# Which engine makes the low halves of three groups of weights in a two-layer hybrid encoder

## The chip, the cores and the metric

The kernel runs on one core of one Trainium2 chip. The metric is the device time of one execution in microseconds (us); the median of three runs before the change is 1833.69 us (1831.79 to 1833.77). Five engines matter: TensorE (PE in the profile, with its weight loads as PEld), VectorE (DVE), ScalarE (ACT), GpSimd (POOL) and SyncE (SP), which here only issues transfers. Each engine works through its own queue of instructions in order, and waits at an instruction until what that instruction needs is there.

## The reference, cut to what matters

Two layers, 512 tokens, 1024 channels. Each layer normalises its input, multiplies it by one wide matrix `w_in`, and feeds the columns to three token mixers whose results are gated and added; a feed-forward block and a gated input embedding follow.

```python
h = rmsnorm(x, norm_mix[i])
proj = h @ w_in[i]
qa, ka, va, glu_in, qc, kc, vc, gates = jnp.split(proj, SPLITS, axis=-1)
ya = diff_attention(qa, ka, va, ...)        # 4 heads, two softmaxes each
yb = conformer_conv(glu_in, ...)            # 31 taps
yc = neighbourhood_attention(qc, kc, vc, ...)   # 8 heads, "natten"
ga, gb, gc = jnp.split(jax.nn.sigmoid(gates), 3, axis=-1)
merged = ga * (ya @ w_br_a[i]) + gb * (yb @ w_br_b[i]) + gc * (yc @ w_br_c[i])
x = x + merged @ w_o[i]
```

All of it is float32.

## The kernel before, in words

Every matrix product runs on TensorE in three parts. An operand is split into a high half, which is the value rounded to the type float32r (fp32r in the profile), and a low half, which is the rest (value minus high half). `mm3` then adds high times high, high times low and low times high. A product with 1024 input channels is eight chunks of 128, so 24 matmuls of 128x512.

Weights come from memory in blocks of 128x1024 float32 (512 KB). `weights` (L162) does this for one block: a transfer on SyncE's queue into the tile `wr` (L167), a copy on ScalarE that makes the high half `wh` (L139, called by `split`), and a subtraction on VectorE that makes the low half `wl` (L153, `tt`, called by `split` at L158). There are two `wr` buffers and three each of `wh` and `wl`, and the whole is put ahead of other work by a priority offset of up to 400, so that a block is prepared while earlier ones are multiplied. The transfer of a block can start only when the low half of the block two before it has been made, because it reuses that `wr` buffer; it is issued from SyncE's queue, where the small copies that arrange queries and keys (`stack`, L582) and the loads of attention biases (L611) are issued too.

`gemm` (L177) multiplies one block and `proj` calls it for a 128-column piece of `w_in`. The name of the stage, `self.phase`, is the prefix of the tile names in the profile: `natten_wl` is the low half of a weight block that was prepared in the stage called natten. One layer runs through glu (the convolution's inputs), natten (queries and keys of four head pairs by `natten_in`, values by `natten_v`), diff (queries and keys of four heads by `diff_in`, values by `diff_v`), gatec (`gate_c`, eight pieces of the third gate), gateb, branchc, mergea, mergeb, wo, ffn and ple. The values' weights go through `values`, which calls `weights` itself and not `gemm`.

The order of TensorE's instructions is written out by hand: attention units (scores, transposes of the probabilities, products with the values) are inserted a number of ticks after the projections that feed them; one tick is four chunks. All other engines' queues are ordered by the framework's planner from its own estimate of times and the priorities. The convolution's taps (L156, `conv_z`, 31 for each of four channel groups in a layer) run on VectorE as background work: some are tied behind certain instructions of each stage (three after every query or key product of natten, one in diff, two in gatec).

VectorE's other work in the stages of the change: scaling the projections (`natten_t`, `gatec_x`), rotary embedding (`diff_rp`), low halves of queries, keys and probabilities (`natten_pt`, `diff_pt`, `natten_a`), bias and row minimum of the scores (L619, `natten_b`), row maxima (L815, `diff_s`), the mixture of the two softmaxes (`diff_a`) and the sum of the attention result (`natten_y`). The tiles named `_mm`, `_sc`, `_tr` and `_av` lie in PSUM, TensorE's result memory; all others lie in SBUF. GpSimd has little to do: it clears 64 columns of some probability tiles (L627) and raises the norms' mean squares to the power -0.5 (L207).

Of the kernel before, what the change touches and what calls it, by code (L numbers as in the profile page):

```python
# [11 lines left out]
F32 = mybir.dt.float32  # L12
F32R = mybir.dt.float32r
I32 = mybir.dt.int32
AF = mybir.ActivationFunctionType
ALU = mybir.AluOpType
# [4 lines left out]
P = 128  # L21
# [36 lines left out]
class Net:  # L58
# [100 lines left out]
        self.act(hi, src, AF.Copy)  # L159
        self.tt(lo, src, hi.bitcast(F32), ALU.subtract)  # L160

    def weights(self, ap, n):  # L162
        with self.tc.high_priority(offset=min(self.w_ahead, self.tc.cur_priority - self.p0)):
            raw = self.sb("wr", [P, 1024])
            hi = self.sb("wh", [P, 1024], F32R)
            lo = self.sb("wl", [P, 1024], F32R)
            self.nc.sync.dma_start(raw[:, :n], ap[:, :n])  # L167
            self.split(hi[:, :n], lo[:, :n], raw[:, :n])
        return hi, lo

    def mm3(self, out, wh, wl, ah, al, first, last):
# [2 lines left out]
        mm(out, wh, al, start=False, stop=False)  # L174
        mm(out, wl, ah, start=False, stop=last)  # L175

    def gemm(self, out, ap, acts, first=True, last=True):  # L177

        n = len(acts)
        for o in range(0, n, 8):  # L180
            c = min(8, n - o)
            wh, wl = self.weights(ap[:, o * P:(o + c) * P], c * P)
            for k in range(c):
                s = slice(k * P, (k + 1) * P)
                h = acts[o + k]
                h = h if isinstance(h, tuple) else (h[:, 0, :], h[:, 1, :])
                self.mm3(out, wh[:, s], wl[:, s], h[0], h[1],
                         first and o + k == 0, last and o + k == n - 1)
                self.chunk()
# [234 lines left out]
    def proj(self, col0, tag="mm"):  # L424
        if self.first:
            return self.first.pop(0)
        ps = self.ps(tag)
        self.gemm(ps, self.a["w_in"][self.i, col0 // P], self.h)
        return ps

    def glu(self, zs):
# [690 lines left out]
```

## Time and profile before

| what | value |
|---|---|
| median of three runs | 1833.69 us |
| the profiled execution's own time | 1832.91 us |
| its span, first to last instruction | 1831.1 us |
| mean granted TensorE clock | 0.999 |
| VectorE busy | 1204.7 us (66%) |
| ScalarE busy | 748.1 us (41%) |
| GpSimd busy | 23.5 us (1%), 56 instructions |
| transfers | 213.80 MB |

The numbers come from one execution. A timeline row gives the start in us, the duration in us, the engine, the line of the kernel, the operation, output and inputs, and in square brackets how long the engine had been idle before it and what ended that. A group row gives the number of instructions, their busy time in us, the mean of one in ns, and the idle time before them with its releasers. Matmuls overlap one another, so their durations are longer than the distance between them.

### The profile page before, as it was taken

Reading aid. Unit: us, or ns where it says so; the run is one execution under the profiler, and the core shown is the slowest. Engines: PE = TensorE matmul, PEld = TensorE weight load, DVE = VectorE, ACT = ScalarE, POOL = GpSimd, SP = SyncE. Lnnn points to the kernel's source line nnn. Section 1 sums busy time; section 2 is a strip of 40 time slices with the busy share of each in tenths; the row PEclk is TensorE's granted clock in tenths of the full one; section 3 lists DMA queues with packets and bytes.
Section 4 is the critical chain, followed back from the end, with each engine's and each line's share of the span. In section 5 each row is a group of like instructions: output and inputs, shape, how many; then the busy total and the mean of one; then the engine's idle time right before and its main releaser. Section 6 shows DMA issues by size and latency. Waiting matters only on the chain.

```text
span 1831.1 us, 23573 instructions
## 1 busy us (share of the span) xinstructions
PE 1815.5 (99%) x8796; PEld 1522.9 (83%) x8796; DVE 1204.7 (66%) x1977; ACT 748.1 (41%) x1280; POOL 23.5 (1%) x56
## 2 busy tenths in 40 slices
PE   9999999999999999999999999999999999999998
PEld 7888888888888888888888888888888888888887
DVE  7788888898544434444767878888985443344455
ACT  5466545334432223233525765442344322223343
POOL 0000000000000000000000000000000000000000
PEclk9999999999999999999999999999999999999999
DMA  5566541334322232222436655322243222322222
GB/s 198 164 189 179 154 118 47 104 103 131 122 93 103 80 113 96 93 90 91 147 114 190 177 157 145 104 69 95 97 150 114 93 93 83 112 102 87 91 90 92
DMA packets 84194, 213.80 MB, mean 117 GB/s; under 512 B 11632, under 2 KB 18928, under 8 KB 84080
## 3 DMA queue, kind: packets, MB, share of 16 engines
q1 hardware_dynamic: 83504, 211.60, 36.8%
q8 instruction: 70, 1.15, 0.2%
q10 hardware_dynamic: 576, 0.69, 0.1%
q14 instruction: 44, 0.36, 0.1%
HBM read 176.59 MB, written 4.19 MB: 99 GB/s over the span
## 4 chain that ended last, share of the span: by engine, by line
PE 91%; DVE 5%; ACT 2%; issue 1%; DMA 1%; SPq 0%; ACTq 0%; DVEq 0%; POOLq 0%; POOL 0%
PE ffn_mm L175 13%; PE ffn_mm L174 13%; PE ffn_mm L173 13%; PE mergea_mm L175 2%; PE mergea_mm L174 2%; PE mergea_mm L173 2%; PE gatec_mm L173 2%; PE wo_mm L174 2%; PE gatec_mm L174 2%; PE gatec_mm L175 2%; PE gateb_mm L174 2%; PE gateb_mm L175 2%; PE wo_mm L175 2%; PE gateb_mm L173 2%; PE wo_mm L173 2%; PE ple_mm L174 2%
## 5 line engine op out<-in xcount | busy, mean ns | idle before, releaser
L139 ACT ACTIVATE ffn_wh<-ffn_wr 128x1024 fp32r<-128x1024 f32 (+1 forms) x152 | 144.7, 952 | 511.4 <-issue 358.3
L173 PE MATMUL ffn_mm<-wo_h,ffn_wh 128*128 128x512 f32 x704 | 274.2, 390 | 0.0
L175 PE MATMUL ffn_mm<-wo_h,ffn_wl 128*128 128x512 f32 x704 | 273.9, 389 | 0.0
L174 PE MATMUL ffn_mm<-wo_h,ffn_wh 128*128 128x512 f32 x704 | 273.9, 389 | 0.0
L153 DVE TENSOR_TENSOR ffn_wl<-ffn_wr,ffn_wh 128x1024 fp32r<-128x1024 f32 (+1 forms) x152 | 164.9, 1085 | 129.4 <-ACT ffn_wh L139 129.4
L156 DVE SCALAR_TENSOR_TENSOR conv_z<-glu_z,pre_par,conv_z 128x512 f32<-128x512 f32 x240 | 179.2, 747 | 1.9
L174 PEld LDWEIGHTS ffn_mm<-wo_h,ffn_wh 128*128 128x128 f32 x704 | 132.1, 188 | 27.5
L173 PEld LDWEIGHTS ffn_mm<-wo_h,ffn_wh 128*128 128x128 f32 x704 | 132.1, 188 | 27.4
L175 PEld LDWEIGHTS ffn_mm<-wo_h,ffn_wl 128*128 128x128 f32 x704 | 132.1, 188 | 27.3
L153 DVE TENSOR_TENSOR ffn_t<-ffn_t,ffn_mm 128x512 f32<-128x512 f32 x44 | 30.3, 688 | 114.8 <-PE ffn_mm L175 114.7
L153 DVE TENSOR_TENSOR ffn_t<-ffn_mm,wo_r 128x512 f32<-128x512 f32 x44 | 30.4, 691 | 111.2 <-PE ffn_mm L175 111.2
L139 ACT ACTIVATE mergea_wh<-mergea_wr 128x1024 fp32r<-128x1024 f32 (+1 forms) x32 | 27.2, 849 | 94.1 <-PE mergea_mm L174 63.1
L173 PE MATMUL ffn_mm<-ffn_z,ffn_wh 128*128 128x512 f32 x160 | 62.2, 389 | 0.0
L174 PE MATMUL ffn_mm<-ffn_z,ffn_wh 128*128 128x512 f32 x160 | 62.2, 389 | 0.0
L175 PE MATMUL ffn_mm<-ffn_z,ffn_wl 128*128 128x512 f32 x160 | 62.2, 389 | 0.0
L173 PE MATMUL ffn_mm<-ffn_y,ffn_wh 128*128 128x512 f32 x160 | 62.2, 389 | 0.0
L174 PE MATMUL ffn_mm<-ffn_y,ffn_wh 128*128 128x512 f32 x160 | 62.2, 389 | 0.0
L175 PE MATMUL ffn_mm<-ffn_y,ffn_wl 128*128 128x512 f32 x160 | 62.2, 389 | 0.0
L139 ACT ACTIVATE diff_a<-diff_sc,diff_s 128x512 f32<-128x512 f32 x32 | 22.0, 689 | 70.7 <-DVE diff_s L815 70.7
L815 DVE TENSOR_REDUCE diff_s<-diff_sc 128x1 f32<-128x512 f32 x64 | 42.1, 685 | 5.4 <-PE diff_sc L725 5.3
L139 ACT ACTIVATE natten_wh<-natten_wr 128x1024 fp32r<-128x1024 f32 x24 | 25.5, 1061 | 47.9 <-PE glu_mm L174 19.9
L153 DVE TENSOR_TENSOR wo_x<-wo_x,ffn_mm 128x512 f32<-128x512 f32 x32 | 22.0, 688 | 34.1 <-PE ffn_mm L175 34.1
(442 smaller groups left out, 4630.9 us busy)
## 6 DMA issues: line engine op xcount, KB each, us to landing
ffn_wr<-w_fg SPq DMA_DIRECT2D x44, 512.0 KB, 3.2
ffn_wr<-w_fu SPq DMA_DIRECT2D x44, 512.0 KB, 3.2
ffn_wr<-w_fd SPq DMA_DIRECT2D x32, 512.0 KB, 3.5
natten_b<-bias SPq DMA_DIRECT2D x32, 256.0 KB, 3.4
natten_wr<-w_in SPq DMA_DIRECT2D x16, 512.0 KB, 3.6
diff_wr<-w_in SPq DMA_DIRECT2D x16, 512.0 KB, 3.9
gatec_wr<-w_in SPq DMA_DIRECT2D x16, 512.0 KB, 3.9
gateb_wr<-w_in SPq DMA_DIRECT2D x16, 512.0 KB, 3.2
```

Of the source, the lines that this page charges most:

```text
L139: i = self.nc.scalar.activation(out, in_, func, **kw)
L153: return self.nc.vector.tensor_tensor(out, a, b, op)
L156: return self.nc.vector.scalar_tensor_tensor(out, a, s, b, op0, op1)
L173: mm(out, wh, ah, start=first, stop=False)
L174: mm(out, wh, al, start=False, stop=False)
L175: mm(out, wl, ah, start=False, stop=last)
L815: nc.vector.tensor_reduce(out=m[:, u:u + 1], in_=sc, op=ALU.max, axis=AX.X, negate=True)
```

## The change

The weight blocks of natten's queries and keys, of the differential attention's queries and keys, and of the gates c get their low half from GpSimd instead of VectorE. The operation is the same (block minus high half). The high half stays on ScalarE. That is eight blocks in each of the three stages of a layer, 48 in all; the values' blocks and every other stage stay as they are.

```diff
-    def weights(self, ap, n):
+    def weights(self, ap, n, pool=False):
...
             self.nc.sync.dma_start(raw[:, :n], ap[:, :n])
-            self.split(hi[:, :n], lo[:, :n], raw[:, :n])
+            if pool:
+                self.act(hi, raw, AF.Copy)
+                self.nc.gpsimd.tensor_tensor(lo, raw, hi.bitcast(F32), ALU.subtract)
+            else:
+                self.split(hi[:, :n], lo[:, :n], raw[:, :n])
         return hi, lo
...
-    def gemm(self, out, ap, acts, first=True, last=True):
+    def gemm(self, out, ap, acts, first=True, last=True, pool=False):
...
-            wh, wl = self.weights(ap[:, o * P:(o + c) * P], c * P)
+            wh, wl = self.weights(ap[:, o * P:(o + c) * P], c * P, pool)
...
-        self.gemm(ps, self.a["w_in"][self.i, col0 // P], self.h)
+        self.gemm(ps, self.a["w_in"][self.i, col0 // P], self.h,
+                  pool=self.phase in ("natten", "diff", "gatec"))
```

In these stages a block always has 1024 columns, so the whole tile in the new branch is the same size as the slice in the old one.

## The prediction

> **What bounds the kernel now.** The page's first part gives the busy time of each engine, and the view by windows that of the two stretches in which the 48 blocks are used (natten, diff and gatec of each layer).
>
> ```profile
> PE 1815.5 (99%) x8796; PEld 1522.9 (83%) x8796; DVE 1204.7 (66%) x1977; ACT 748.1 (41%) x1280; POOL 23.5 (1%) x56
> ...
> 40.00:300.00 260.00, 257.26 (x1488) 223.49 (x1487) 219.22 (x457) 142.60 (x316) 5.15 (x17) 1.00 0.51 147
> 945.00:1207.00 262.00, 258.63 (x1492) 224.23 (x1491) 216.67 (x446) 142.38 (x316) 5.15 (x17) 1.00 0.50 143
> ```
>
> TensorE is busy 1815.5 of 1831.1 us, and its matmuls are untouched. So the change can win only where TensorE is idle: 260 - 257.26 = 2.74 us in the first stretch and 262 - 258.63 = 3.37 us in the second, **6.1 us together**, 0.33% of the time. VectorE is busy 219.22 of 260 us, 84%, so its queue can be late there. Next the view of waits, for TensorE alone, in the two stretches (total, times, longest).
>
> ```profile
> PE natten_av L663 <- DVE natten_y L153: 1.0, 3, 0.6
> PE natten_sc L725 <- DVE natten_s L619: 1.0, 1, 1.0
> PE diff_tr L211 <- DVE diff_pt L153: 0.6, 1, 0.6
> ...
> PE natten_av L663 <- DVE natten_y L153: 1.4, 4, 0.7
> PE natten_sc L725 <- DVE natten_s L619: 1.0, 1, 1.0
> PE diff_tr L211 <- DVE diff_pt L153: 0.6, 1, 0.6
> ```
>
> These make 5.6 us, all of them waits for VectorE: 2.4 for `natten_y`, 2.0 for `natten_s`, 1.2 for `diff_pt`. What put VectorE behind is read from the chain of waits, whose pieces with a low half of the 48 blocks are these (start, length).
>
> ```profile
> 96.39 1.13 DVE natten_wl L153
> ...
> 127.17 1.14 DVE diff_wl L153
> ...
> 136.56 1.14 DVE diff_wl L153
> ...
> 220.69 1.23 DVE gatec_wl L153
> ...
> 1001.43 1.23 DVE natten_wl L153
> ...
> 1017.68 1.23 DVE natten_wl L153
> ...
> 1033.15 1.14 DVE diff_wl L153
> ...
> 1042.55 1.14 DVE diff_wl L153
> ...
> 1127.04 1.23 DVE gatec_wl L153
> ```
>
> Nine of the 48 lie on the path that sets the end. The timeline shows the plainest case: a low half stands between two score instructions, and TensorE waits for the second because it needs the score buffer back.
>
> ```profile
> 136.48 1.22 DVE L153 TENSOR_TENSOR diff_wl<-diff_wr,diff_wh 128x1024 fp32r<-128x1024 f32 x1
> 137.62 0.41 DVE L619 CUSTOM_DVE_ANT_0 natten_b<-natten_sc,natten_b 128x256 f32<-128x256 f32 x1
> 138.10 0.39 PE L725 MATMUL natten_sc<-natten_qk 128*128 128x256 f32 x1 [0.97 <-DVE natten_s L619]
> ```
>
> **The change part by part.** *Removed from VectorE:* 48 subtractions, eight each in natten, diff and gatec of two layers.
>
> ```profile
> L153 DVE TENSOR_TENSOR diff_wl<-diff_wr,diff_wh 128x1024 fp32r<-128x1024 f32 x12 | 14.7, 1223 | 4.6 <-ACT diff_wh L139 4.5
> ```
>
> 48 x 1.22 = 58.6 us of VectorE's time, 29.3 in each stretch (the twelve of this row include four blocks of the values, which stay). VectorE falls from 219 to 190 of 260 us, 73%. Off the path that is worth nothing; on it, the nine pieces are worth what TensorE waited behind them. The 2.0 us for `natten_s` have a `diff_wl` of 1.14 directly before the late instruction, more than either wait of 1.0: all 2.0 go. Of the 2.4 us for `natten_y`, the 0.6 (the longest of the first layer, near 95 us) has no low half between its start in a TensorE result and its end; the other six have one: 1.8 go. The 1.2 us for `diff_pt` hang on the two `gatec_wl`, and there I take nothing, for the reason below.
>
> *Added on GpSimd:* 48 subtractions of 128x1024 with two inputs. This trace has no such instruction on GpSimd. The nearest rows are its fills and one selection.
>
> ```profile
> L627 POOL MEMSET natten_e<- 128x64 f32 x32 | 4.7, 152 | 283.5 <-ACT natten_e L139 139.8 <-PE natten_tr L644 120.4 <-ACT natten_y L139 9.7
> ...
> masks.py:199 POOL TENSOR_SCALAR_AFFINE_SELECT pre_ident<-pre_ident 128x128 f32<-128x128 f32 x1 | 0.3, 293 | 0.1
> masks.py:197 POOL MEMSET pre_ident<- 128x128 f32 x1 | 0.2, 204 | 0.3 <-POOLq L1111 0.3
> ...
> L1111 POOL MEMSET const-float32-1.0<- 128x1 f32 x1 | 0.1, 99 | 0.0
> ```
>
> A fill costs 0.10 us and (204 - 99) / 127 = 0.8 ns a column; the selection, one read and one write, (293 - 99) / 127 = 1.5 ns. A second read at the 0.7 between them makes 2.2 to 2.3 ns, so 0.1 + 1024 x 2.25 = **2.4 us** as my estimate. Bounds: not below VectorE's 1.22, and at most three passes at the selection's 1.5 ns, 4.7 us. I take 2.4 as it is nearest to the selection's row. 24 in a stretch keep GpSimd busy 58 us (29 to 113) of 260, so it doesn't saturate. [...]
>
> *Latency of the low half.* It is hidden by the lead of the blocks.
>
> ```profile
> 94.64 1.06 ACT L139 ACTIVATE natten_wh<-natten_wr 128x1024 fp32r<-128x1024 f32 x1 [0.45 <-PE natten_mm L174]
> ...
> 96.30 1.22 DVE L153 TENSOR_TENSOR natten_wl<-natten_wr,natten_wh 128x1024 fp32r<-128x1024 f32 x1
> ...
> 97.55 0.33 SPq L167 DMA_DIRECT2D natten_wr<-w_in  x1
> ...
> 102.71 1.06 ACT L139 ACTIVATE natten_wh<-natten_wr 128x1024 fp32r<-128x1024 f32 x1 [2.21 <-PE natten_mm L174]
> ```
>
> A high half starts when TensorE lets go of the buffer of the block three before, 8.1 us after the previous one; two more blocks are multiplied before the new one is due, about 16 us. High half 1.06 plus 2.4 (or 4.7) leaves 10 us. Without that cover the cost would be up to 2.4 - 1.2 = 1.2 us a block, 58 us over all 48. I take nothing. *SyncE's queue* does wait: the next load of weights (97.55) goes out when the low half ends (97.52), 1.82 us after the high half (95.70). With GpSimd that is 2.4, so 0.6 later (2.9 at the upper bound), and the copies of queries and keys issued behind it (L582) shift too. The transfer itself isn't missed, since its block is due two blocks later. I take nothing and keep 0.6 a block for a rival. Behind a low half on GpSimd wait the fills of 0.15 us (no TensorE wait names them) and the norms' powers; a power waits up to 2.4 us and has a tick or two before TensorE needs it. Nothing for these either.
>
> *Contention.* VectorE and GpSimd get in each other's way in this trace. GpSimd's power instruction takes 1.01 us beside a VectorE reduction that reads PSUM, and 1.32 us when it comes while VectorE subtracts or adds two SBUF tiles (the same 1.32 in the other layer).
>
> ```profile
> 288.83 0.69 DVE L815 TENSOR_REDUCE diff_s<-diff_sc 128x1 f32<-128x512 f32 x1
> ...
> 288.99 1.01 POOL L207 TENSOR_TENSOR diff_rc<-diff_sm,pre_power 128x4 f32<-128x4 f32 x1 [29.31 <-DVE diff_sm L156]
> ...
> 318.86 0.69 DVE L153 TENSOR_TENSOR conv_ss<-conv_z,conv_z 128x512 f32<-128x512 f32 x1
> ...
> 319.09 1.32 POOL L207 TENSOR_TENSOR diff_rc<-diff_sm,pre_power 128x4 f32<-128x4 f32 x1 [29.09 <-DVE diff_sm L156]
> ```
>
> The 0.31 us more is about what was left of the VectorE instruction (318.86 + 0.69 - 319.09 = 0.46). So GpSimd waits for a VectorE instruction with two SBUF inputs; whether VectorE waits for GpSimd in turn no row shows, since GpSimd reads only four columns here. Bounds for one such meeting: nothing, or the rest of a 2.4 us subtraction. [...]
>
> VectorE's instructions with two SBUF inputs in the first stretch are above all these.
>
> ```profile
> L156 DVE SCALAR_TENSOR_TENSOR conv_z<-glu_z,pre_par,conv_z 128x512 f32<-128x512 f32 x56 | 41.7, 744 | 0.1
> ...
> L156 DVE SCALAR_TENSOR_TENSOR diff_a<-diff_e,diff_s,diff_a 128x512 f32<-128x512 f32 x15 | 11.2, 749 | 0.3
> ...
> L153 DVE TENSOR_TENSOR diff_rp<-diff_rp,diff_r 128x512 f32<-128x512 f32 x16 | 11.0, 687 | 0.1
> ...
> 221.83 0.68 DVE L153 TENSOR_TENSOR diff_rp<-diff_rp,diff_kh 128x512 fp32r<-128x512 f32 x1
> ```
>
> They make 63.9 us, with the smaller ones some 85 of the 190 that stay, 45%. In the natten chains what follows a low half reads PSUM (`natten_b` at 137.62, then `natten_y` and `natten_pt`), so GpSimd's 2.4 us pass beside it. Behind `gatec_wl` at 220.69 comes `diff_rp` with two SBUF inputs: it would be held until 220.69 + 2.4 = 223.1 and not start at 221.8. That is why the 1.2 us for `diff_pt` are counted as kept.
>
> **Sum.** 2.0 + 1.8 = 3.8 us off the profiled execution's 1832.91 (span 1831.1 and 1.8 around it) gives 1829.1. The median of the runs shown is 0.8 above that execution; I give **1829.5**, within the middle of the two.
>
> **The rivals.**
> 1. *All idle time goes:* without contention the `diff_pt` waits and the rest vanish too: 1832.9 - 6.1 = 1826.8. For it: every wait named is VectorE's. Against it: ScalarE's hi copies and exponentials stand in the same chains.
> [...]
> [...]
> 4. *Slower, by SyncE's queue:* 0.6 us later copies of queries and keys in the seven natten chains, 4.2 us: 1837.1. Against it: no TensorE wait in the list is for a transfer.
>
> That GpSimd does nothing of this is excluded, as the engine is named in the call.
>
> **How the numbers follow.** Forecast 0.37, rival 1 0.08, rival 2 0.27, rival 3 0.23, rival 4 0.05. A measurement of this kernel tells about 0.2% (3.7 us) from no change. Forecast and rival 1 count as faster, 0.45; rival 2 as same, 0.27; rivals 3 and 4 as slower, 0.28. The forecast's own range is 1827 to 1831.5. The range for 8 in 10 goes from 1826.5 (rival 1 less the scatter of the runs) to 1839.5 (rival 3 with the natten chains unharmed, and a us of scatter); the worse half of rival 3 is left out.
>
> **What would show it.** Right: TensorE's two waits for `natten_s` are gone, those for `natten_y` fall from 2.4 to about 0.6, TensorE's idle time in the two stretches is near 2.3 us; GpSimd's subtractions take about 2.4 us; `natten_pt` and `natten_b` keep their durations. [...] It is wrong if new TensorE waits for low halves, for `natten_qk` copies or for GpSimd's powers appear, or if the planner has put other work into the freed places so that the same waits stay with another instruction in front.

## The result, and the profile after

The kernel with the change takes **1854.93 us** (median of 4 runs, 1853.84 to 1855.67) against 1833.73 for the kernel before (4 runs, 1831.79 to 1833.89): ratio 1.0118, 95% interval 1.0100 to 1.0135. It is 21.2 us slower, outside the range that was given. The span of the profiled execution is 1853.5 us at a mean granted clock of 0.996.

The first part of the profile's page after (busy time, share, instructions):

```profile
PE 1821.5 (98%) x8796; PEld 1526.3 (82%) x8796; DVE 1204.9 (65%) x1929; ACT 746.5 (40%) x1280; POOL 143.7 (8%) x104
```

VectorE has 48 instructions fewer and yet the same busy time, 1204.9 us against 1204.7. Everything that was taken off it has come back inside its other instructions. The two stretches of the 48 blocks after, in the view by windows (length; busy us and count of PE, PEld, DVE, ACT, POOL; granted clock, DMA share, GB/s):

```profile
40.00:300.00 260.00, 248.95 (x1418) 214.75 (x1417) 210.82 (x415) 137.06 (x305) 64.98 (x42) 0.99 0.50 145
960.00:1225.00 265.00, 253.79 (x1459) 220.00 (x1458) 209.99 (x415) 138.70 (x309) 64.76 (x43) 0.99 0.49 141
```

TensorE stands idle for 11.05 and 11.21 us where it was 2.74 and 3.37 before. Its waits after (total, times, longest):

```profile
PE diff_tr L203 <- ACT diff_ss L139: 5.2, 2, 2.7
PE diff_tr L216 <- DVE diff_pt L153: 4.3, 2, 2.1
PE natten_av L669 <- DVE natten_y L153: 3.2, 7, 0.8
PE natten_sc L731 <- DVE natten_s L625: 2.1, 2, 1.1
PE natten_av L669 <- ACT natten_e L139: 2.1, 2, 1.0
PE natten_tr L650 <- ACT natten_e L139: 1.3, 1, 1.3
```

`diff_pt` has grown from 1.2 to 4.3, `natten_y` from 2.4 to 3.2, and a wait that did not exist, for `diff_ss`, is the longest of all. The row for `natten_s` (2.1 for 2.0) looks like the old one but isn't: the two score products that waited at 138.10 and 1044.08 us before no longer wait, as was forecast, and two others, at 172.80 and 1089.34, now do. The rows of the first of them (start, duration; in square brackets the idle time before):

```profile
165.53 2.39 POOL L170 TENSOR_TENSOR diff_wl<-diff_wr,diff_wh 128x1024 fp32r<-128x1024 f32 x1 [6.30 <-ACT diff_wh L139]
...
167.95 0.33 SPq L167 DMA_DIRECT2D diff_wr<-w_in  x1
...
168.33 0.91 SPq L617 DMA_DIRECT2D natten_b<-bias  x2
...
172.31 0.42 DVE L625 CUSTOM_DVE_ANT_0 natten_b<-natten_sc,natten_b 128x256 f32<-128x256 f32 x1 [1.04 <-DMA natten_b<-bias]
...
172.80 0.39 PE L731 MATMUL natten_sc<-natten_qk 128*128 128x256 f32 x1 [1.15 <-DVE natten_s L625]
```

No held VectorE instruction stands in this chain: the block's load goes out when GpSimd is done, the attention's biases stand behind it in SyncE's queue, VectorE waits for the biases and TensorE for VectorE.

The groups that stand for VectorE's work in the first stretch after, at the same place where the prediction showed `conv_z` at 744 ns and `diff_rp` at 687:

```profile
L156 DVE SCALAR_TENSOR_TENSOR conv_z<-glu_z,pre_par,conv_z 128x512 f32<-128x512 f32 x54 | 53.5, 990 | 0.2
L153 DVE TENSOR_TENSOR diff_rp<-diff_rp,diff_r 128x512 f32<-128x512 f32 x16 | 15.6, 977 | 2.9 <-DMA diff_rp<-diff_rp 2.9
L625 DVE CUSTOM_DVE_ANT_0 natten_b<-natten_sc,natten_b 128x256 f32<-128x256 f32 x32 | 12.4, 419 | 1.7 <-DMA natten_b<-bias 1.5
L153 DVE TENSOR_TENSOR natten_pt<-natten_tr,natten_pt 128x512 fp32r<-128x512 f32 x16 | 11.0, 686 | 3.8 <-ACT natten_pt L139 3.6
```

On the mean these two groups with two SBUF inputs are a third to two fifths longer (990 ns for 744, 977 for 687), while `diff_a` is not (752 for 749); those with one input in PSUM have kept their times to 2 ns (`natten_b` 419 for 420, `natten_pt` 686 for 688). The mean hides that most have not changed and a few are held long. The taps by their line (shortest/median/longest in ns), before and after:

```profile
L156 DVE SCALAR_TENSOR_TENSOR conv_z<-glu_z,pre_par,conv_z x240: 731/747/756, 39.9 to 1306.6; 128x512 f32<-128x512 f32 x120
```

```profile
L156 DVE SCALAR_TENSOR_TENSOR conv_z<-glu_z,pre_par,conv_z x240: 727/747/2987, 39.8 to 1328.7; 128x512 f32<-128x512 f32 x120
```

Set against the medians of the kernel before, 33 of VectorE's 1929 instructions are longer by more than 0.06 us, by 52.5 us together and by 2.24 at most. All 33 read two SBUF tiles. Beside them 89 others with at most one SBUF input began while one of the subtractions ran, 61 of these with an input in PSUM, and kept their times to 0.01 us. The groups of GpSimd's subtractions after, over the whole execution:

```profile
L170 POOL TENSOR_TENSOR natten_wl<-natten_wr,natten_wh 128x1024 fp32r<-128x1024 f32 x16 | 41.2, 2573 | 133.1 <-ACT natten_wh L139 117.3 <-PE natten_av L670 15.8
L170 POOL TENSOR_TENSOR gatec_wl<-gatec_wr,gatec_wh 128x1024 fp32r<-128x1024 f32 x16 | 39.8, 2490 | 70.1 <-ACT gatec_wh L139 70.1
L170 POOL TENSOR_TENSOR diff_wl<-diff_wr,diff_wh 128x1024 fp32r<-128x1024 f32 x16 | 39.6, 2475 | 136.0 <-ACT diff_wh L139 136.0
```

How one hold looks, and how it becomes a stall of TensorE, is read from the timeline after:

```profile
212.47 0.75 DVE L156 SCALAR_TENSOR_TENSOR conv_z<-glu_z,pre_par,conv_z 128x512 f32<-128x512 f32 x1
212.54 2.94 POOL L170 TENSOR_TENSOR diff_wl<-diff_wr,diff_wh 128x1024 fp32r<-128x1024 f32 x1 [18.84 <-ACT diff_wh L139]
...
213.60 1.89 DVE L156 SCALAR_TENSOR_TENSOR diff_s<-diff_s,glu_nlam,diff_sm 128x1 f32<-128x1 f32 x1
...
220.59 2.99 DVE L156 SCALAR_TENSOR_TENSOR conv_z<-glu_z,pre_par,conv_z 128x512 f32<-128x512 f32 x1
220.62 2.41 POOL L170 TENSOR_TENSOR diff_wl<-diff_wr,diff_wh 128x1024 fp32r<-128x1024 f32 x1 [5.15 <-ACT diff_wh L139]
...
228.11 2.61 POOL L170 TENSOR_TENSOR gatec_wl<-gatec_wr,gatec_wh 128x1024 fp32r<-128x1024 f32 x1 [5.08 <-ACT gatec_wh L139]
228.97 2.29 DVE L153 TENSOR_TENSOR diff_rp<-diff_rp,diff_rp 128x512 f32<-128x512 f32 x1
...
231.19 0.68 DVE L821 TENSOR_REDUCE diff_s<-diff_sc 128x1 f32<-128x512 f32 x1
...
231.83 0.67 ACT L139 ACTIVATE diff_a<-diff_sc,diff_s 128x512 f32<-128x512 f32 x1
...
232.50 0.68 ACT L139 ACTIVATE diff_e<-diff_sc,diff_s 128x512 f32<-128x512 f32 x1
...
233.16 0.59 ACT L139 ACTIVATE diff_ss<-diff_av 128x512 f32<-128x512 f32 x1
...
233.81 0.66 PE L203 MATMUL diff_tr<-pre_ident,diff_ss 128*128 128x128 f32 x4 [2.68 <-ACT diff_ss L139]
```

At 220.6 a convolution tap begins 0.03 us before GpSimd's subtraction and ends 0.55 us after it: 2.99 us for 0.75. At 213.6 an instruction on a single column, normally 0.22 us, takes 1.89. The tap at 212.47 shows the other order: it began 0.07 us ahead of GpSimd's subtraction, keeps its 0.75 us, and the subtraction takes 2.94 us, where the shortest take 2.36. At 228.97 a rotation of the rotary embedding is held, 2.29 for 0.68. Behind it in VectorE's queue stands the row maximum, behind that on ScalarE the two exponentials, behind those the copy `diff_ss`, and TensorE waits 2.68 us for that copy. None of these instructions has anything to do with a weight.

A further cost appears right behind that stall, in the view by windows of the same place after (the granted clock is the number after the busy times):

```profile
230.00:234.00 4.00, 1.32 (x7) 0.78 (x7) 3.49 (x7) 2.70 (x7) 0.72 (x1) 1.00 0.21 49
234.00:235.00 1.00, 1.00 (x7) 0.88 (x7) 0.78 (x2) 1.00 (x3) 0.00 (x0) 0.86 0.86 197
235.00:236.00 1.00, 1.00 (x4) 0.80 (x3) 1.00 (x3) 0.42 (x2) 0.00 (x0) 0.50 0.94 219
236.00:237.00 1.00, 1.00 (x4) 0.74 (x3) 1.00 (x4) 0.11 (x1) 0.22 (x1) 0.50 0.91 213
237.00:238.00 1.00, 1.00 (x4) 0.81 (x3) 0.90 (x2) 0.66 (x2) 0.79 (x1) 0.50 1.04 295
238.00:240.00 2.00, 2.00 (x11) 1.63 (x11) 1.11 (x3) 1.21 (x5) 0.00 (x0) 0.97 0.73 222
```

TensorE is busy in all of 234 to 240 us, but it has lost 0.14 + 3 x 0.50 + 2 x 0.03 = 1.7 us of clock. The same happens at 173 to 177 us and, in the second layer, at 1149 to 1153, 1.7 us each time; the kernel before shows no such drop in the two stretches. The span of this execution is 22.4 us longer than before: 16.2 are TensorE's additional idle time in the two stretches, and up to 5.1 are its slower clock.

### The profile page after: what moved, and what is told of

It is laid out like the page before. It is cut to its first block, busy times and chain, and to the rows that moved or that the text cites. A ratio compares the mean times of both kernels' runs of the same rounds, so it can differ in the third digit from the quotient of the medians.

```text
span 1853.5 us, 23571 instructions
## 1 busy us (share of the span) xinstructions
PE 1821.5 (98%) x8796; PEld 1526.3 (82%) x8796; DVE 1204.9 (65%) x1929; ACT 746.5 (40%) x1280; POOL 143.7 (8%) x104
## 3 DMA queue, kind: packets, MB, share of 16 engines
q8 instruction: 70, 1.15, 0.2%
## 4 chain that ended last, share of the span: by engine, by line
PE 83%; DVE 9%; ACT 2%; issue 2%; DMA 2%; SPq 1%; POOL 0%; DVEq 0%; POOLq 0%; ACTq 0%
PE ffn_mm L178 13%; PE ffn_mm L179 13%; PE ffn_mm L177 13%; DVE conv_z L156 3%; PE mergea_mm L177 2%; PE mergea_mm L179 2%; PE mergea_mm L178 2%; DVE diff_rp L153 2%; PE wo_mm L178 2%; PE gateb_mm L179 2%; PE gateb_mm L178 2%; PE gateb_mm L177 2%; PE wo_mm L179 2%; PE wo_mm L177 2%; PE ple_mm L177 2%
## 5 line engine op out<-in xcount | busy, mean ns | idle before, releaser
L156 DVE SCALAR_TENSOR_TENSOR conv_z<-glu_z,pre_par,conv_z 128x512 f32<-128x512 f32 x240 | 203.3, 847 | 2.0
L170 POOL TENSOR_TENSOR natten_wl<-natten_wr,natten_wh 128x1024 fp32r<-128x1024 f32 x16 | 41.2, 2573 | 133.1 <-ACT natten_wh L139 117.3
L170 POOL TENSOR_TENSOR diff_wl<-diff_wr,diff_wh 128x1024 fp32r<-128x1024 f32 x16 | 39.6, 2475 | 136.0 <-ACT diff_wh L139 136.0
```

What stands on the lines that cost most here:

```text
L156: return self.nc.vector.scalar_tensor_tensor(out, a, s, b, op0, op1)
L170: self.nc.gpsimd.tensor_tensor(lo, raw, hi.bitcast(F32), ALU.subtract)
```

## The experiments

**The theories.** T1, called port in the expectations: while GpSimd's subtraction reads, VectorE's instructions with two SBUF inputs stand still, and that lateness reaches TensorE; what in the chip makes them stand still is not shown by any run. Its rivals: T2, the blocks are late, because GpSimd needs 2.4 us where VectorE needs 1.2 (and with them what stands behind their loads in SyncE's queue); T3, the planner's new order of VectorE's and ScalarE's queues is at fault. Differences in time below are by the ratios, times 1833 us.

**1. The relief without the reads.** GpSimd fills the low half and the load buffer and reads nothing; VectorE's and ScalarE's orders are those of the change but for four places.

```diff
             if pool:
                 self.act(hi, raw, AF.Copy)
-                self.nc.gpsimd.tensor_tensor(lo, raw, hi.bitcast(F32), ALU.subtract)
+                self.nc.gpsimd.memset(lo.bitcast(F32), 0.0)
+                self.nc.gpsimd.memset(raw, 0.0)
+                self.nc.gpsimd.memset(raw[:, :512], 0.0)
```

> GpSimd no longer subtracts: behind each of the 48 high halves it fills the low half (1024 columns) and then overwrites the block it came from (1024 and 512 columns), so it is busy about as long (2560 columns at 0.8 ns and 0.1 us each, 2.4 us) and holds the block's buffer as long, but reads nothing; the product of high and low parts of those weights is left out. The queues of VectorE and ScalarE stand as in the changed kernel but for four places, SyncE's nearly so. Theory port (a VectorE instruction with two SBUF inputs stands still while a GpSimd instruction reads SBUF, and the other way round): no VectorE instruction is stretched, the longest conv_z is back at 0.76 us, and the time falls from 1854.9 to 1828 to 1833. Theory order (the planner put the queues of VectorE, ScalarE and SyncE in a worse order): stays at 1850 to 1856. Theory late blocks (GpSimd's 2.4 us instead of 1.2 delays SyncE's next loads): stays at 1848 or more, since the buffer is released as late.

Measured: 1830.81 us, ratio 0.9985 (0.9976 to 0.9995). The page's first part, and the row of `conv_z` by its line (min/median/max in ns):

```profile
PE 1814.1 (99%) x8796; PEld 1524.5 (83%) x8796; DVE 1153.8 (63%) x1929; ACT 745.8 (41%) x1280; POOL 138.5 (8%) x200
```

```profile
L156 DVE SCALAR_TENSOR_TENSOR conv_z<-glu_z,pre_par,conv_z x240: 728/745/755, 41.1 to 1305.6; 128x512 f32<-128x512 f32 x120
```

GpSimd is as busy as with the change (138.5 and 143.7 us), VectorE has the change's order, and no tap takes more than 755 ns. VectorE's busy time falls by 50.9 us and the time by 2.8. That is what the relief is worth here, and T3 falls as an explanation of the loss. Against the change this kernel differs by 51.1 us of VectorE's time and 24.4 us of the whole, which are the price of the reads, unless late blocks have a part in it.

**2. The reads without the relief.** VectorE keeps all its work, in exactly the order of the kernel before; GpSimd in addition subtracts twice 480 columns of each high half into a tile that nobody reads.

```diff
             if pool:
-                self.act(hi, raw, AF.Copy)
-                self.nc.gpsimd.tensor_tensor(lo, raw, hi.bitcast(F32), ALU.subtract)
+                self.split(hi, lo, raw)
+                s = self.sb("scr", [P, 480])
+                for c in range(0, 960, 480):
+                    h = hi[:, c:c + 480].bitcast(F32)
+                    self.nc.gpsimd.tensor_tensor(s, h, h, ALU.subtract)
...
-                         e=4, a=3, r=4, ss=1, sm=8, rc=4, b=2, s=8)
+                         e=4, a=3, r=4, ss=1, sm=8, rc=4, b=2, s=8, scr=1)
```

> The kernel before, VectorE makes all low halves, and GpSimd in addition reads 960 of the 1024 columns of each of the 48 high halves (two subtractions of 480 columns, both inputs the high half, into a scratch tile that nobody reads). The queues of VectorE, ScalarE and SyncE stand exactly as before, and nothing waits for the scratch. Theory port: VectorE loses what it lost in the changed kernel (58 us in all) without being relieved of its 58 us, so the time is well above 1855, 1870 to 1900. Theories order and late blocks: within 2 us of the kernel before, 1832 to 1836.

Measured: 1857.35 us, ratio 1.0133 (1.0116 to 1.0150). The same two views:

```profile
PE 1826.1 (98%) x8796; PEld 1522.6 (82%) x8796; DVE 1243.5 (67%) x1977; ACT 746.0 (40%) x1280; POOL 167.8 (9%) x152
```

```profile
L156 DVE SCALAR_TENSOR_TENSOR conv_z<-glu_z,pre_par,conv_z x240: 728/745/1479, 39.6 to 1329.6; 128x512 f32<-128x512 f32 x120
```

No block waits for GpSimd, no queue is reordered, and the time rises by 24.4 us, with VectorE 38.8 us busier. Not all of it is T1's. Set instruction by instruction against the kernel before, TensorE loses 2.0 us between 310 and 930 us and 1.7 us from 1215 us on, in stages with none of the 48 blocks; some products `wo_mm` of L180 take 395 ns there for 389. The change loses nothing in these stages. So 3.7 us came with the edit but not with a held VectorE instruction; what makes them stays open. Some 20.7 us are left, so T1 is enough for most of the loss by itself. The size that was expected, 1870 to 1900, was too large: it took the held time for lost time.

**3. Shorter holds.** The change, with the subtraction cut into four of 256 columns.

```diff
-                self.nc.gpsimd.tensor_tensor(lo, raw, hi.bitcast(F32), ALU.subtract)
+                for c in range(0, 1024, 256):
+                    q = slice(c, c + 256)
+                    self.nc.gpsimd.tensor_tensor(lo[:, q], raw[:, q], hi[:, q].bitcast(F32), ALU.subtract)
```

> The changed kernel with each of GpSimd's subtractions cut into four of 256 columns; the queues of VectorE, ScalarE and SyncE stand exactly as in the changed kernel. Theory port, held for a whole instruction: a VectorE instruction is held 0.7 us at most instead of 2.4 and gets in between two pieces, longest conv_z about 1.5 us instead of 2.99, low halves later; 1838 to 1848. Theory order: 1854 to 1858. Theory late blocks: slower than 1855, since four instructions take longer than one.

Measured: 1853.74 us, ratio 1.0108 (1.0093 to 1.0123), outside the 1838 to 1848 us that were expected of T1.

```profile
PE 1819.8 (98%) x8796; PEld 1524.4 (82%) x8796; DVE 1182.6 (64%) x1929; ACT 746.4 (40%) x1280; POOL 193.0 (10%) x248
```

```profile
L156 DVE SCALAR_TENSOR_TENSOR conv_z<-glu_z,pre_par,conv_z x240: 730/747/1242, 39.8 to 1324.6; 128x512 f32<-128x512 f32 x120
```

The holds are shorter (the longest tap 1.24 us and not 2.99), and VectorE is held 28.8 us (over experiment 1) and not 51.1, but the time is nearly that of the change. The last piece of a block is ready 3.6 us after its high half on the mean and 4.8 at most, against 2.6 with the change, so late blocks (T2) come into question.

**4. Late blocks alone.** As experiment 1, with the load buffer held longer behind the high half and nothing read: three fills (shown), and four.

```diff
             if pool:
+                self.nc.gpsimd.memset(lo.bitcast(F32), 0.0)
                 self.act(hi, raw, AF.Copy)
-                self.nc.gpsimd.tensor_tensor(lo, raw, hi.bitcast(F32), ALU.subtract)
+                self.nc.gpsimd.memset(raw, 0.0)
+                self.nc.gpsimd.memset(raw, 0.0)
+                self.nc.gpsimd.memset(raw, 0.0)
```

> As the fill, but after each of the 48 high halves GpSimd overwrites the block it came from three times (3 x 0.95 us), so the block's buffer comes free 2.9 us after the high half, later than in the changed kernel (2.6 us in the mean) and than in the first fill (about 1.6); nothing is read by GpSimd, and the product of high and low parts of those weights is left out. VectorE's and ScalarE's queues differ from the changed kernel's in 30 and 6 places. Theory port alone: as the fill, 1829 to 1833. Theory late blocks (the loads of weights, and the bias loads and copies behind them on SyncE's queue, come later): the more of the changed kernel's 21 us it explains, the nearer to 1855; half would be 1842.

> Like e1_fill (GpSimd clears the low half and reads nothing, so the 48 blocks are multiplied without a low half of their own), but the block's load buffer is cleared four times behind the high half, so it is released about 3.8 us after the high half, where the kernel of the change has 2.6 us on the mean and e3_pieces about 3.6 to 4.8. This asks whether the lateness of the blocks explains why e3_pieces stayed at 1853.7 although it held VectorE half as long. If lateness is the cause: 1845 us or more. If it is not (the loads still come in time): 1829 to 1834, and the price of e3_pieces lies in the number of holds or their place rather than in late blocks.

Measured: 1831.27 us (0.9987, 0.9978 to 0.9996) and 1834.87 us (1.0002, 0.9993 to 1.0012). With the gaps between the fills, the load buffer is released 3.0 and 4.1 us after the high half on the mean; it is 2.6 with the change and 1.6 in experiment 1. At 3.0 us it costs 0.4 us over experiment 1, less than can be told. At 4.1 us it costs 3.1 us by the ratios, a step that neither theory had expected. The experiment only asks when the buffer is let go, since these kernels have the low half early; but with the change too every low half is ready 7.2 us or more before TensorE's first product with it.

This doesn't clear T2 altogether, because the planner gave these kernels another order of SyncE's queue. With three fills the biases are sent at 162.29 us, ahead of the block's load at 164.88, while with the change they stand behind the load. That is where the change waits at 172.80 and 1089.34 us: 1.15 and 0.92 us, and the first is followed by a drop of the clock (1.7 us). Experiment 1 has the change's order there, releases the buffer about 1 us earlier, and TensorE waits 0.2 us at most. So up to 3.8 of the 22.4 us that the change's profiled execution is longer belong to T2.

**5. One stage at a time.** The change in natten, in diff, or in gatec alone.

```diff
-                  pool=self.phase in ("natten", "diff", "gatec"))
+                  pool=self.phase == "natten")
```

> Only natten's 16 blocks go to GpSimd. By the shifts of TensorE's instructions between the two traces, natten costs 3.0 us in the first layer and 0.7 in the second, the stages of diff the rest. Theory port: 1834 to 1839, a small loss, since natten's VectorE work is mostly reads of PSUM. Theory order: about a third of the loss, 1839 to 1843. My forecast's part for natten's own blocks would have been 1831 to 1833.

> Only the differential attention's 16 blocks go to GpSimd. Theory port: this is where VectorE's two-input work is dense (rotary embedding, mixture, taps), and where TensorE's instructions shift most; 1840 to 1847. Theory that each block costs the same: natten alone cost 2.4 us for 16 blocks, so 1836.

> Only the gates c's 16 blocks go to GpSimd. Theory port: 1838 to 1845; with natten's 2.4 us and the differential attention's part the three should add up to about 21 us if the parts are independent, and to less if a hold costs more where another one has already used up the slack.

Measured: natten 1836.0 us (1.0013, 1.0003 to 1.0022), diff 1841.44 (1.0043, 1.0028 to 1.0058), gatec 1843.77 (1.0060, 1.0043 to 1.0077). In us that is 2.4 + 7.9 + 11.0 = 21.3, close to the 21.6 of all three together (0.0118 x 1833): the costs add. They don't follow how long VectorE is held. Its busy time is 1204.2, 1203.3 and 1207.4 us; taking a third of experiment 1's relief (17.0 us) off the 1204.7 of before, it is held 16.5, 15.6 and 19.7 us. What differs is what waits behind a hold. With gatec alone TensorE's waits for `diff_pt` grow from 1.2 to 8.0 us, and two of them are followed by a drop of the clock of 1.7 us: 10.2 of its 11.0 us. With diff alone TensorE waits 0.85 and 0.92 us for score products whose biases stand behind a late load, as in experiment 4's case, and a drop of 1.7 us follows each: up to 5.2 of its 7.9 us, so that in this stage the late loads (T2) may weigh more than the holds.

**6. Other doses of the same hold.** The kernel before, order kept, with one extra subtraction of 480 columns for each block instead of two; and with two copies (one input) of 480 columns instead of the two subtractions. Each cut is set against experiment 2.

```diff
-                for c in range(0, 960, 480):
+                for c in range(0, 480, 480):
...
-                    self.nc.gpsimd.tensor_tensor(s, h, h, ALU.subtract)
+                    self.nc.gpsimd.tensor_copy(s, hi[:, c:c + 480].bitcast(F32))
```

> The kernel before with all its VectorE work, order kept; GpSimd additionally copies two pieces of 480 columns of each high half into a scratch tile that nobody reads: one input instead of the two of e2_dummy, and the scratch is again the only output. If any read by GpSimd holds VectorE's instructions with two SBUF inputs: 1843 to 1857 us, with conv_z instructions of over 1.0 us. If only GpSimd instructions with two inputs hold VectorE: 1831 to 1836, and conv_z stays below 0.8 us.

> Like e2_dummy, with one extra subtraction of 480 columns on GpSimd for each of the 48 blocks instead of two; VectorE keeps all its work and the order of before. e2_dummy lost 23.8 us in time for 38.8 us more of VectorE's busy time, 0.61 us per us; e10_copy 9 for 14.2, 0.65. If the price follows the time that VectorE is held: 19 us more of VectorE's busy time and 1845 to 1847. If a slack ahead of the stalls takes up the first part: 1839 or less. If the number of blocks touched decides and not the time they are held: 1851 or more.

Measured: copies 1843.10 us (1.0051, 1.0035 to 1.0067), one subtraction 1843.06 (1.0057, 1.0040 to 1.0073). The rows of `conv_z`, first with the copies, then with the one subtraction:

```profile
L156 DVE SCALAR_TENSOR_TENSOR conv_z<-glu_z,pre_par,conv_z x240: 729/746/1072, 39.4 to 1311.9; 128x512 f32<-128x512 f32 x120
```

```profile
L156 DVE SCALAR_TENSOR_TENSOR conv_z<-glu_z,pre_par,conv_z x240: 729/747/1480, 39.8 to 1315.2; 128x512 f32<-128x512 f32 x120
```

A copy that reads one tile holds VectorE too (the longest tap by 1072 - 745 = 327 ns), so reading one tile was enough for a hold, where a fill made none (755 ns at most in experiment 1). One subtraction fell some 2 us short of its expectation; VectorE was held for 16.0 us and not 19. Both kernels, like experiment 2, lose time in the stages with none of the 48 blocks, 2.0 and 1.5 us, whatever the dose. The fourth column of the table is that part, and the price of a held us is worked out without it.

| kernel | VectorE held, us | slower by, us | of it elsewhere, us | per us held |
|---|---|---|---|---|
| copies over before | 1218.9 - 1204.7 = 14.2 | 9.3 | 3.5 | 0.41 |
| one subtraction over before | 1220.7 - 1204.7 = 16.0 | 10.4 | 3.5 | 0.43 |
| two subtractions over before | 1243.5 - 1204.7 = 38.8 | 24.4 | 3.7 | 0.53 |
| pieces over experiment 1 | 1182.6 - 1153.8 = 28.8 | 22.6 | none | 0.78 |
| the change over experiment 1 | 1204.9 - 1153.8 = 51.1 | 24.4 | none | 0.48 |

A small dose costs too, so there is no slack that takes up the first 14 us. Whether a held us costs more in a large dose can't be told: the times of the first two rows are uncertain by some 3 us each. The price of the change, with VectorE relieved of 48 subtractions, is much the same as with its work kept. The pieces' 0.78 falls to (22.6 - 3.1) / 28.8 = 0.68 when the late blocks of experiment 4 are taken off; they too have the wait behind late biases (1.52 us at 175.12, followed by a drop of the clock), but why it isn't 0.48 stays open.

**7. Two tries for a faster kernel without GpSimd.** The low halves stay on VectorE: first with a priority offset of 100 in place of 400, so that other work goes ahead of them; then as two subtractions of 512 columns.

```diff
-            self.split(hi[:, :n], lo[:, :n], raw[:, :n])
+            self.act(hi[:, :n], raw[:, :n], AF.Copy)
+        late = 100 if self.phase in ("natten", "diff", "gatec") else self.w_ahead
+        with self.tc.high_priority(offset=min(late, self.tc.cur_priority - self.p0)):
+            self.tt(lo[:, :n], raw[:, :n], hi[:, :n].bitcast(F32), ALU.subtract)
```

```diff
-            self.split(hi[:, :n], lo[:, :n], raw[:, :n])
+            if self.phase in ("natten", "diff", "gatec") and n == 1024:
+                self.act(hi, raw, AF.Copy)
+                for c in (0, 512):
+                    s = slice(c, c + 512)
+                    self.tt(lo[:, s], raw[:, s], hi[:, s].bitcast(F32), ALU.subtract)
+            else:
+                self.split(hi[:, :n], lo[:, :n], raw[:, :n])
```

> The kernel before, with the 48 low halves still on VectorE, but their subtraction put only 100 places ahead of its turn instead of 400 (high halves and loads stay at 400), so that the planner lets VectorE do score and probability work first. GpSimd does nothing new. If the low halves stand in the way of more urgent work, as the chain of waits of before says, up to 6 us of TensorE's idle time can go: 1828 to 1832. If the blocks' buffers come free too late for the next load then: 1835 or more.

> The kernel before, but each of the 48 low halves is made on VectorE as two subtractions of 512 columns, so that a score instruction waits for 0.7 us instead of 1.2. This is a try for a faster kernel that leaves the port alone. If the nine low halves on the path cost what they last: their share of the relief measured by e1_fill (2.8 us) is half recovered, 1831 to 1833. If the planner's order decides (as in e8_late, where another order alone cost 4 us): 1834 to 1840. The extra instruction costs 48 x 0.1 to 0.2 us of VectorE's time.

Measured: 1837.68 us (1.0024, 1.0015 to 1.0034), and 1835.50 us (1.0010, 1.0000 to 1.0019). Behind other work the low half comes up to 8.6 us after its high half, and TensorE's instructions shift by 5.8 us near 175 to 181 us. Two halves gain nothing either. No kernel that computes the whole reference beat the one before; even experiment 1, which leaves the low halves out, is only 0.15% faster.

## Why the prediction was wrong, step by step

- **What can be won, 6.1 us of TensorE's idle time.** As a limit of a gain it stood: the relief alone brought 2.8. But the step had no limit for a loss, and the idle time in the two stretches rose from 6.1 to 22.3 us.
- **3.8 us for nine low halves on the path.** The size was off: 2.8. In experiment 1 the waits for `natten_s` and for `diff_pt` were gone, the second of which had been counted as kept, but the one for `natten_y` grew from 2.4 to 3.9, where 0.6 was forecast. So a wait that goes in one place can come back a few instructions on: where the first layer waited 0.97 us for `natten_s` at 138.10, experiment 1 waits 0.81 and 0.39 for `natten_y`, at 141.30 and 145.77. Here is its row among the waits of experiment 1:

```profile
PE natten_av L671 <- DVE natten_y L153: 3.9, 8, 0.8
```

- **2.4 us for GpSimd's subtraction.** Right: 2.48 to 2.57 on the mean, 2.36 to 2.39 the shortest.
- **Latency and SyncE's queue, nothing.** Right for the low half itself, which is ready 7.2 us or more before its first use. Wrong for SyncE's queue, which was booked as nothing: at 172.80 and 1089.34 us it passes the block's lateness on, through the biases that stand behind the load. That is 2.1 us of waits, and with the drop of the clock behind the first of them up to 3.8. Rival 4 had this mechanism, for the copies of queries and keys, and its 4.2 us are near; it had against it that no TensorE wait is for a transfer, but here VectorE waits for the transfer and TensorE for VectorE. As the only cause it is rejected: experiment 2, in which no load waits for GpSimd, loses some 20.7 us all the same.
- **Contention. This is the step that failed.** The prediction saw the exclusion from GpSimd's side (1.32 us for 1.01), left VectorE's side open, and then asked only which of the nine low halves on the old path are followed by two-input work. Two was the answer (the `gatec_wl`), and 1.2 us were booked as kept. But a hold needs no low half on the old path. 33 of the 48 subtractions held the two-input instruction that VectorE had next, and in diff and gatec, where TensorE had waited 1.2 us in all, that made new chains such as the one at 228.97. Experiments 1 and 2 show it from both ends: without the reads 24.4 us go (up to 3.8 of them T2's), and the reads alone cost some 20.7. The 1.2 us of `diff_pt` booked as kept became 4.3 in the change and 8.0 with gatec alone. The longest tap tells the same: 755 ns where GpSimd only wrote (experiment 1), 1479 where it read 480 columns at a time (experiment 2), and 2.99 us beside the change's subtraction of 1024.
- **The natten chains unharmed.** Right for the instructions (`natten_b` 419 ns, `natten_pt` 686), and natten is the cheapest stage, but it was to bring the whole gain and cost 2.4 us. Its rotations (`natten_t`) and the taps between the chains are two-input work, and VectorE is held there as long as in diff (16.5 and 15.6 us).
- **Rival 2, the same time.** It said that holds take from VectorE just what it is relieved of, and that sum was right almost to the digit: VectorE lost 51.1 us to holds for 50.9 us of relief. What followed from it was wrong. Equal busy time isn't equal lateness. The reason, argued from the timeline and not tried by itself: a low half has its place in the planner's order, while a hold of up to 2.2 us falls on any two-input instruction, such as the rotation at 228.97, whose successors were to run at once.
- **Rival 3, slower by holds.** The right sign and the main mechanism, the second with no row of before behind it; the price of 5.4 to 10.8 us was too small by half or more, and its condition, that GpSimd takes more than 2.4 us, was wrong. It took 3.55 us for GpSimd's subtraction, the middle of 2.4 and 4.7, charged a hold net of the relief (3.55 - 1.2 - 1.2, about 1.2 us) and only at nine places, so that 2.4 us came out as the point of no loss. The upper end of the range, 1839.5, stands on this net hold, which no run shows: over the 48 blocks there are 51.1 us of holds for 50.9 of relief, net nothing, and a loss all the same. At 2.4 us GpSimd's reads, with the late loads, cost 24.4 us, 0.5 for each of the 48 blocks, and the relief gives 2.8 back.

## What to carry to other kernels

Before work goes to GpSimd, look at what VectorE does meanwhile: here VectorE instructions with two SBUF inputs that came while GpSimd's subtraction read SBUF stood still until it was done (33 of them, by 0.2 to 2.24 us), and each us so held cost 0.4 to 0.5 us of the whole time (0.7 to 0.8 with the pieces), while 51 us taken off VectorE were worth 2.8. Price such a change over the whole stretch in which the two engines overlap, not over the places that are on the path now, and never net the holds against the relief. Fills on GpSimd, which only write, held no tap here (755 ns at most), and VectorE's instructions with an input in PSUM kept their times (`natten_b` 419 ns for 420). Look as well at what stands behind a load in SyncE's queue when the load waits for the slower engine: here the biases behind it made TensorE wait 1.15 and 0.92 us.

## What was not expected of the hardware

- A hold ended with GpSimd's subtraction, whatever the size of VectorE's instruction: one column took 1.89 us for 0.22 and ended 0.02 us after the subtraction, a whole tile took 2.99 for 0.75 and ended 0.55 us after it. So it was with all 33 (0.02 us for the two single columns, 0.55 to 0.56 for the others).
- It went both ways, and the one that started first was not held. In 22 places a VectorE instruction with two SBUF inputs began 0.03 to 0.57 us ahead of GpSimd's subtraction, as at 212.47; it kept its time, and GpSimd took 2.43 to 2.97 us instead of 2.36 to 2.39. Of the 33 that were held, 32 began after GpSimd's had begun; the tap at 220.59 is recorded 0.03 us ahead of it.
- Three times in the change the granted clock falls to 0.50 for 3.41 us (1.7 us lost each). Two of the drops come right behind stalls of TensorE of 2.68 and 2.48 us, the third behind three waits of 0.33, 0.27 and 1.15 us close together. The length of a stall doesn't decide it alone: two stalls of 2.14 us in the change have no drop behind them, and two of 2.14 and 2.15 us with gatec alone have one each. What sets a drop off is not shown. The dummy of experiment 2, with a clock of 0.999, lost its time without such drops.
- Cutting GpSimd's instruction was dear: a piece of 256 columns took 0.89 to 0.94 us on the mean, so four of them 3.6 to 3.8 us against 2.5 for the whole. Part of that may be waiting for VectorE between the pieces, since two in a row took 1.41 us at 172.96, 0.7 each.
